# A two-layer decoder trunk on Trainium2: side-token gelu, index pieces and selection steps placed differently in the expert layers

## The chip, the core and the metric

The kernel runs on one core of one Trainium2 chip. The metric is the device time of one execution in microseconds (us). A core has five engines that run side by side, each with its own instruction queue worked off in order: PE (TensorE, matrix products), DVE (VectorE), ACT (ScalarE), POOL (GpSimd) and SP (SyncE, which here only issues transfers). DMA engines move data between HBM and the on-chip memory. An engine whose next instruction waits for another engine holds up everything behind it in its queue.

## What is computed

The reference is a trunk of two layers on 512 tokens of width 1024. Each layer has a mixer (gated linear attention in layer 1, stick-breaking attention in layer 2, both with cross-attention into 256 memory tokens) and a PEER expert layer, each followed by a layer norm. The change touches the expert layers alone. There, for each token:

```python
q = (xf @ w_q).reshape(N, PEER_HEADS, 2, PEER_QHALF)           # 8 heads, 2 halves of 128
s = jnp.einsum('nhpd,hpkd->nhpk', q, subkeys)                  # 128 scores per half
top_s, top_i = lax.top_k(s, PEER_TOPK)                         # 16 best of each half
cand_s = top_s[:, :, 0, :, None] + top_s[:, :, 1, None, :]     # 16 x 16 sums
best_s, best_pos = lax.top_k(cand_s.reshape(N, 8, 256), PEER_TOPK)
idx = jnp.take_along_axis(cand_i, best_pos, axis=-1)           # 128 experts of 16384
g = jax.nn.softmax(best_s, axis=-1)
act = jax.nn.gelu(jnp.einsum('nd,nhkd->nhk', xt, u_tab[it]))   # their products with x
out = jnp.einsum('nhk,nhkd->nd', gt * act, v_tab[it])          # weighted sum of v rows
```

## The kernel before, in words

**Two ways to the experts.** Tokens lie in four tiles of 128. For most tokens the kernel computes the products with *all* 16384 experts (the U stage, 128 blocks of 128 experts each), turns the chosen experts' weights into a dense matrix of gates, and multiplies by all rows of the V table (the V stage, 128 blocks). Tile 0, the gathered tile, instead fetches its 128 chosen rows per token with indirect DMA from POOL, from the U table and then from the V table. The first 16 tokens of tile 1, the side tokens, have their U products gathered too, but take part in the V stage. `SD` is 16, `T0` is 128 and `TU` is 368, the tokens whose U products are dense.

**The U stage.** The loop over `b` (L1605 on) issues for each block, in this order: `prep` loads the block two ahead and splits it into a high and a low part (`uh` on ACT, L97; `ul` on DVE, L98, issued a little later through `later`); `stat_mm` multiplies, 24 matmuls on PE (L117 to L119, tile `ph`); ACT applies gelu to the previous block's products (L1620 or L1622); then five streams of smaller work each get their share. A buffer ring of three holds the split parts.

**The streams.** A `Stream` holds generators and a credit `c`. A call adds a number of nanoseconds to `c` (at most twice that number stands there afterwards) and runs generator steps as long as `c` is above zero. Each step yields its assumed cost, which is subtracted; a step that yields `None` sets `c` to zero and ends the call. So the costs written in the `yield` lines decide in which block a piece is issued. The streams are:

- `gst`: the gates. Each step scales one-hot rows on ACT (`obl`, L1486), every second one makes new one-hot rows on DVE (`ob`, L1457 and L1463), and a step's products go to PE (`pg`, L1505 and L1506) one step later and through ACT (`gt`, L1509) to DRAM (`Gd`, L1511, issued from ACT's queue). The credit is 1.25 a block, so every fourth block has two steps. First come tile 1's gates without the side tokens, then the side tokens' (`side_gates`), then tiles 2 and 3.
- `lead`: the selection of the gathered tile. While the queries are made, `select` lets `topk16` work on one row of scores at a time for up to three tiles; after that `first_rest` does what is left: the last row (`stage1`), the last candidates (`stage2`), the indices of heads 4 to 7 (`indices`), and the softmax.
- `work`: the same for tiles 1, 2 and 3 (`rest`), with `gate_prep`, and `side_prep` for the side tokens. It runs only when `lead` is empty, with 1000 ns a block once gates can be made (`WB`), else 1700 (`WB0`).
- `gus`: the gathered products. A step of `gather_u` multiplies one gathered row per token on DVE (L1156, with its sum) and issues the next gather on POOL (L1103). After the last side product `side_late` is started, and each later step of `gather_u` runs it one `yield` further. `gather_v` follows, mostly in the V stage.

**Index operations.** `indices` turns positions among the candidates into expert numbers with fifteen short DVE operations (L1263 to L1278), then for four heads at a time two broadcasts on ACT (`tb`, L1286), two compares (L1290), two products (L1293) and a tree of sums (L1297, L1299) on DVE.

**`side_late`** applies gelu to the side products on ACT (L1384), multiplies by the softmax weights on DVE (L1386), sends them through DRAM (`Sw`, out and back on SP's queue) to another layout, transposes them on PE and makes three bf16 parts `wb`, for which `side_gates` waits.

**The V stage** (L1702 on) loads gates and V rows, forms `w` = gate times activation (L1694 on DVE, L1696 on ACT for the side tokens' gates), splits it (`whi` L1698, `wlo` L1699), splits the V rows, and multiplies into six accumulators (L285 to L289). Its first gates, those of U blocks 112 to 117, are loaded by SP into `g0`, a view of the tile the trace names `keep` or `big` (L1659). DVE, ACT and PE carry orders written out by hand inside each stage; a planner places the instructions of successive stages against each other, and orders SP's and POOL's.

Of the kernel before, what the change touches and what calls it, by code (L numbers as in the profile page):

```python
# [1052 lines left out]
def peer(E, mixer, wq, sk, ut, vt, un, lng, lnb, out_dram=None, follow=()):  # L1053
# [10 lines left out]
    with ExitStack() as pp:  # L1064
# [118 lines left out]
        with ExitStack() as up:  # L1183
# [8 lines left out]
            def topk16(*jobs):  # L1192

                for v, i, s, s2 in jobs:
                    nc.vector.max(v[:, 0:8], s)
                for v, i, s, s2 in jobs:
                    nc.vector.match_replace(s2, v[:, 0:8], s, -3.4e38)
                for v, i, s, s2 in jobs:
                    nc.vector.max_index(i[:, 0:8], v[:, 0:8], s)
                for v, i, s, s2 in jobs:  # L1200
                    nc.vector.max(v[:, 8:16], s2)
                for v, i, s, s2 in jobs:
                    nc.vector.max_index(i[:, 8:16], v[:, 8:16], s2)

            class Sel:
# [16 lines left out]

                def stage1(self):

                    topk16(*[self.job() for _ in range(min(2, avail[0] - self.nr))])
                    return 2350

                def stage2(self):

# [23 lines left out]
                def indices(self, h0=0, h1=8):  # L1253

                    n = (h1 - h0) * 16
                    ih = min(4, h1 - h0)
                    sh = wk.tile([P, P], U32, tag="sh", name="sh", bufs=1)[:, :n]
                    af = wk.tile([P, P], F32, tag="af", name="af", bufs=1)[:, :n]
                    bf = wk.tile([P, P], F32, tag="bf", name="bf", bufs=1)[:, :n]
                    ab = wk.tile([P, 2, P], F16, tag="ab", name="ab", bufs=1)  # L1260
                    st = sh.bitcast(F32)
                    tif = wk.tile([P, 16, 16], F16, tag="tif", name="tif", bufs=1)[:, 2 * h0:2 * h1]
                    nc.vector.tensor_copy(tif, self.top_i[:, 2 * h0:2 * h1])  # L1263
                    pf = self.pos[:, h0:h1].rearrange("p h k -> p (h k)")
                    nc.vector.tensor_scalar(sh, pf, 4, None, op0=ALU.logical_shift_right)
                    nc.vector.tensor_copy(af, sh)
                    nc.vector.tensor_scalar(sh, pf, 3, None, op0=ALU.logical_shift_right)
                    nc.vector.scalar_tensor_tensor(af, sh, -1.0, af, op0=ALU.add, op1=ALU.max)
                    nc.vector.tensor_scalar(sh, pf, 2, None, op0=ALU.logical_shift_right)
                    nc.vector.scalar_tensor_tensor(af, sh, -6.0, af, op0=ALU.add, op1=ALU.max)  # L1270
                    nc.vector.scalar_tensor_tensor(af, pf, -48.0, af, op0=ALU.add, op1=ALU.max)
                    nc.vector.tensor_scalar(st, af, 8.0, 8.0, op0=ALU.mult, op1=ALU.add)
                    nc.vector.scalar_tensor_tensor(bf, af, 16.0, st, op0=ALU.mult, op1=ALU.min)
                    nc.vector.tensor_scalar(st, af, 4.0, 24.0, op0=ALU.mult, op1=ALU.add)
                    nc.vector.tensor_tensor(bf, bf, st, op=ALU.min)
                    nc.vector.scalar_tensor_tensor(bf, af, 48.0, bf, op0=ALU.add, op1=ALU.min)
                    nc.vector.tensor_sub(ab[:, 1, :n], pf, bf)
                    nc.vector.tensor_copy(ab[:, 0, :n], af)  # L1278
                    yield 1000 + 10 * n
                    tv = tif.rearrange("p (h two) k -> p two h k", two=2)  # L1280
                    for h in range(0, h1 - h0, ih):
                        hs = slice(h, h + ih)
                        tb, eq = [], []
                        for half in range(2):
                            tb.append(wk.tile([P, 4, 16, 16], F16, tag=f"tb{half}", name="tb", bufs=1)[:, :ih])
                            nc.scalar.activation(tb[half], tv[:, half, hs, :, None].to_broadcast([P, ih, 16, 16]), AF.Copy)  # L1286
                        for half in range(2):
                            eq.append(wk.tile([P, 4, 16, 16], F16, tag=f"eq{half}", name="eq", bufs=1)[:, :ih])
                            av = ab[:, half, :n].rearrange("p (h k) -> p h k", k=16)
                            nc.vector.tensor_tensor(eq[half], av[:, hs, None, :].to_broadcast([P, ih, 16, 16]),  # L1290
                                                    E.iota16[:, None].to_broadcast([P, ih, 16, 16]), op=ALU.is_equal)
                        for half in range(2):
                            nc.vector.tensor_mul(eq[half], eq[half], tb[half])  # L1293
                        yield 700 * ih
                        for m in (8, 4, 2):
                            for e in eq:
                                nc.vector.tensor_add(e[:, :, 0:m], e[:, :, 0:m], e[:, :, m:2 * m])  # L1297
                        for half, e in enumerate(eq):
                            nc.vector.tensor_add(self.i12[:, half, h0 + h:h0 + h + ih], e[:, :, 0], e[:, :, 1])  # L1299
                        yield 500 * ih  # L1300
# [80 lines left out]
            def side_late():  # L1381

                sh, sg, sw = side["sh"], side["sg"], side["sw"]
                nc.scalar.activation(sh, sh, AF.Gelu)  # L1384
                yield
                nc.vector.tensor_mul(sh, sh, sg)  # L1386
                nc.sync.dma_start(Sw.rearrange("h t k -> (h t) k"), sh)
                for _ in range(3):
                    yield
                nc.sync.dma_start(sw[:SD].rearrange("t (h k) -> t h k", h=8), Sw.rearrange("h t k -> t h k"))  # L1390
                for _ in range(3):
                    yield
                pt = psum(E, name="gts")
                nc.tensor.transpose(pt[:, :SD], sw[:SD], E.ident[:SD, :SD])
                yield
                wb = tp.tile([P, 3, SD, 2], BF16, name="wb")
                ws = tp.tile([P, 2, SD], F32, name="ws")
                nc.vector.tensor_copy(ws[:, 0], pt[:, :SD])
                for k in range(3):
                    nc.vector.tensor_copy(wb[:, k], ws[:, 0, :, None].to_broadcast([P, SD, 2]))  # L1400
                    if k < 2:
                        nc.vector.tensor_copy(ws[:, 1], wb[:, k, :, 0])
                        nc.vector.tensor_sub(ws[:, 0], ws[:, 0], ws[:, 1])
                sready.append(wb)

            def side_gates():

                while not sready:
                    yield 1
                wb = sready[0]  # L1410
                pairs = lambda ap: ap.rearrange("p q (i two) -> p q i two", two=2)
                gt = wk.tile([P, P, TS], F32, tag="gt", name="gt")
                todo, ev = None, None
                for step in range(2 * SD // OT + 1):
                    n = step * OT // 2
                    if ev:
                        ev()
                        ev = None
                    if todo:
                        ev = side_mm(*todo)  # L1420
                        todo = None
                    elif n < SD:
                        if n % DT == 0:
                            ob = onehots(siT, None, n)
                        part = ob[:, n % DT:n % DT + OT]
                        e = pairs(part[:, :, 0])
                        ol = []
                        for k in (1, 2, 0):
                            o = e
                            if k > 0:  # L1430
                                ol.append(wk.tile([P, OT, P], F16, tag="obl", name="obl").bitcast(BF16))
                                o = pairs(ol[-1])
                            nc.vector.tensor_tensor(o, e, wb[:, k, n:n + OT, None, :].to_broadcast([P, OT, P // 2, 2]), op=ALU.mult)
                        todo = (n, gt, part, ol)
                    yield GR
# [79 lines left out]
            avail = [0]  # L1515
# [35 lines left out]
            lead = Stream()  # L1551
# [49 lines left out]
            avail[0] = 16  # L1601
            lead.q.append(first_rest())
            gst = Stream(gates(list(range(SD, P, OT))), side_gates(), gates(2 * list(range(0, P, OT))))
            ab, ph, later = None, None, []
            for b in range(P + 1):  # L1605
                if b == KB:
# [226 lines left out]
```

## Time and profile before

| | us |
|---|---|
| median of 3 runs | 2884.08 |
| lowest and highest run | 2877.16, 2887.15 |
| profiled execution, own time | 2882.44 |
| its span, first to last instruction | 2880.7 |
| PE busy | 2840.5 |
| DVE busy | 2407.6 |
| ACT busy | 1450.8 |

The U stage of layer 1 runs from 336 us to 913 us of the span, that of layer 2 from 1769 to 2346. In a timeline row the first number is the start in us from the span's beginning, the second the duration; then follow engine, line, operation, what it writes from what, the shapes, and how many such instructions the row merges. In square brackets stands how long the engine idled before it and what ended that. A row of waits reads: engine, waiting tile and line, what it waited for, us in total, how many times, the longest. A row of windows gives, after the stretch and its length, the busy time of PE, PE's weight loads, DVE, ACT and POOL, the granted clock of PE, the share of the DMA engines and GB/s.

### The profile page before, as it was taken

The numbers are of one execution on the slowest core, as the hardware profiler recorded it, in microseconds if no ns is written. First come the engines' busy times: TensorE is split into PE (matmuls) and PEld (weight loads), VectorE is DVE, ScalarE is ACT, GpSimd is POOL, SyncE is SP. The second block draws the span as 40 slices with busy tenths as digits, with TensorE's granted clock in tenths as the row PEclk, the third lists the DMA queues.
The fourth block names the chain that finished last, engine by engine and source line by source line (L and its number), as shares of the span: only waits on it lengthen the run. The fifth ranks groups of instructions, "written<-read, shape, count | busy, mean of one in ns | idle before, by whom it ended". The sixth has DMA issues, their size and how long they took to land. (4 is left out here: it accounts for less than half of the span.)

```text
span 2880.7 us, 44606 instructions
## 1 busy us (share of the span) xinstructions
PE 2840.5 (99%) x16144; PEld 2512.2 (87%) x16144; DVE 2407.6 (84%) x4944; ACT 1450.8 (50%) x2723; POOL 796.0 (28%) x584
## 2 busy tenths in 40 slices
PE   9999999999999999999999999999999999999998
PEld 7888899899999888888877788998999998888886
DVE  5567999899876888788868779998998778888888
ACT  6342447657674343344445424466676733344432
POOL 0100243233334333353000002432333333333330
PEclk9999999999999999999999999999999999999999
DMA  5232498899999999999521325988999999999994
GB/s 192 102 110 71 167 325 314 299 321 333 346 351 376 329 364 379 366 366 379 195 79 52 110 81 187 326 316 297 326 333 346 350 376 325 354 376 385 375 365 159
DMA packets 311070, 806.87 MB, mean 280 GB/s; under 512 B 32176, under 2 KB 124480, under 8 KB 304448
## 3 DMA queue, kind: packets, MB, share of 16 engines
q1 hardware_dynamic: 195936, 414.93, 41.3%
q0 software_dynamic: 78336, 285.25, 27.2%
q10 hardware_dynamic: 36576, 103.85, 9.4%
q8 instruction: 126, 2.06, 0.3%
q14 instruction: 96, 0.79, 0.1%
HBM read 708.19 MB, written 94.68 MB: 279 GB/s over the span
## 5 line engine op out<-in xcount | busy, mean ns | idle before, releaser
L117 PE MATMUL ph<-xhi,uh 128*128 128x368 f32 x2048 | 689.5, 337 | 0.0
L119 PE MATMUL ph<-xhi,ul 128*128 128x368 f32 x2048 | 677.5, 331 | 7.3 <-DVE ul L98 7.1
L118 PE MATMUL ph<-xlo,uh 128*128 128x368 f32 x2048 | 675.2, 330 | 0.0
L1103 POOL DMA_INDIRECT gr<-in_un,gidx x256 | 387.5, 1514 | 826.7 <-DVE gr L1156 599.4
L1103 POOL DMA_INDIRECT gr<-in_vt,gidx x256 | 334.7, 1307 | 610.5 <-DVE va L1175 530.3
L97 ACT ACTIVATE vh<-vr 128x1024 fp32r<-128x1024 f32 x256 | 271.2, 1060 | 427.7 <-PE acc L289 311.9
L285 PE MATMUL acc<-vh,whi 128*128 128x512 f32 x1536 | 473.8, 390 | 1.5 <-ACT whi L1698 1.5
L287 PE MATMUL acc<-vl,whi 128*128 128x512 f32 x1536 | 473.6, 389 | 0.1
L289 PE MATMUL acc<-vh,wlo 128*128 128x512 f32 x1536 | 473.3, 389 | 0.0
L98 DVE TENSOR_TENSOR vl<-vr,vh 128x1024 fp32r<-128x1024 f32 x256 | 313.0, 1223 | 157.4 <-ACT vh L97 156.0
L97 ACT ACTIVATE uh<-ur 128x1024 fp32r<-128x1024 f32 x288 | 303.9, 1055 | 204.4 <-PE ph L118 178.2
L119 PEld LDWEIGHTS ph<-xhi,ul 128*128 128x128 f32 x2048 | 386.1, 189 | 13.5 <-DVE ul L98 13.5
L98 DVE TENSOR_TENSOR ul<-ur,uh 128x1024 fp32r<-128x1024 f32 x288 | 351.1, 1219 | 47.7 <-ACT uh L97 46.4
L118 PEld LDWEIGHTS ph<-xlo,uh 128*128 128x128 f32 x2048 | 386.9, 189 | 0.0
L117 PEld LDWEIGHTS ph<-xhi,uh 128*128 128x128 f32 x2048 | 386.6, 189 | 0.1
L285 PEld LDWEIGHTS acc<-vh,whi 128*128 128x128 f32 x1536 | 287.6, 188 | 63.0 <-ACT whi L1698 3.7
L287 PEld LDWEIGHTS acc<-vl,whi 128*128 128x128 f32 x1536 | 287.8, 188 | 61.3 <-DVE vl L98 1.8
L289 PEld LDWEIGHTS acc<-vh,wlo 128*128 128x128 f32 x1536 | 287.7, 188 | 61.1 <-DVE wlo L1699 1.6
L1156 DVE SCALAR_TENSOR_TENSOR gr<-gr,xnat 128x1024 f32<-128x1024 f32 x256 | 310.0, 1217 | 24.8 <-DMA gr<-in_un,gidx 24.6
L1175 DVE SCALAR_TENSOR_TENSOR va<-gr,gw,va 128x1024 f32<-128x1024 f32 x254 | 325.1, 1280 | 3.8 <-DMA gr<-in_vt,gidx 2.7
L1486 ACT ACTIVATE obl<-ob,rat 128x128 f16<-128x128 f16 x736 | 234.3, 392 | 33.6 <-ACT gt L1509 16.2
L1698 ACT ACTIVATE whi<-w 128x384 fp32r<-128x384 f32 x256 | 132.2, 516 | 141.6 <-DVE w L1694 140.7
(358 smaller groups left out, 4100.0 us busy)
## 6 DMA issues: line engine op xcount, KB each, us to landing
ur<-in_ut SPq DMA_DIRECT2D x256, 512.0 KB
vr<-in_vt SPq DMA_DIRECT2D x256, 512.0 KB
Gd<-gt ACTq DMA_DIRECT2D x48, 1024.0 KB
Ad<-act ACTq DMA_DIRECT2D x112, 368.0 KB
al<-Ad SPq DMA_DIRECT2D x112, 368.0 KB
gl<-Gd SPq DMA_DIRECT2D x26, 1536.0 KB
ur<-in_wq SPq DMA_DIRECT2D x32, 512.0 KB
bs<-in_b_st SPq DMA_DIRECT2D x14, 512.0 KB
```

Of the source, the lines that this page charges most:

```text
L97: nc.scalar.activation(hi, raw, AF.Copy)
L98: sub = lambda: eng.tensor_sub(lo, raw, hi.bitcast(F32))
L117: nc.tensor.matmul(ps, h, xhi[:, c, sl], start=(c == 0), stop=False)
L118: nc.tensor.matmul(ps, h, xlo[:, c, sl], start=False, stop=False)
L119: nc.tensor.matmul(ps, l, xhi[:, c, sl], start=False, stop=(c == NC - 1))
L285: nc.tensor.matmul(acc[hf], lh, hi[:, hf * 512:(hf + 1) * 512], start=first, stop=False)
L287: nc.tensor.matmul(acc[hf], lh, lo[:, hf * 512:(hf + 1) * 512], start=False, stop=False)
L289: nc.tensor.matmul(acc[hf], ll, hi[:, hf * 512:(hf + 1) * 512], start=False, stop=last)
L1103: nc.gpsimd.indirect_dma_start(out=gr, out_offset=None, in_=tab, in_offset=bass.IndirectOffsetOnAxis(ap=idx[:, k:k + 1], axis=0))
L1156: nc.vector.scalar_tensor_tensor(gr, gr, 1.0, xr, op0=ALU.mult, op1=ALU.mult, accum_out=dst[:, k:k + 1])
L1175: nc.vector.scalar_tensor_tensor(va, gr, gw[:, k:k + 1], va, op0=ALU.mult, op1=ALU.add)
L1486: nc.scalar.activation(obl[:, q], ob[:, q, 0], AF.Copy, scale=rat[:, n0 + q:n0 + q + 1])
```

## The change

Four things are done. In `side_late` two more `yield` lines stand ahead of the gelu, so it is issued two steps of `gather_u` later. In `indices` the fifteen operations are cut in two pieces of eight and seven, the compares and the products become pieces of their own, and the assumed costs are other numbers. In `stage1` the assumed cost goes by the number of rows, 1200 ns each, instead of 2350 for any number. And ahead of the U loop the credit of `lead` is set to -2000, whatever it was.

```diff
                 def stage1(self):
-                    topk16(*[self.job() for _ in range(min(2, avail[0] - self.nr))])
-                    return 2350
+                    jobs = [self.job() for _ in range(min(2, avail[0] - self.nr))]
+                    topk16(*jobs)
+                    return 1200 * len(jobs)
...
                     nc.vector.scalar_tensor_tensor(af, pf, -48.0, af, op0=ALU.add, op1=ALU.max)
+                    yield 700 + 11 * n
                     nc.vector.tensor_scalar(st, af, 8.0, 8.0, op0=ALU.mult, op1=ALU.add)
...
                     nc.vector.tensor_copy(ab[:, 0, :n], af)
-                    yield 1000 + 10 * n
+                    yield 600 + 10 * n
...
                                                     E.iota16[:, None].to_broadcast([P, ih, 16, 16]), op=ALU.is_equal)
+                        yield 300 * ih
                         for half in range(2):
                             nc.vector.tensor_mul(eq[half], eq[half], tb[half])
-                        yield 700 * ih
+                        yield 300 * ih
...
                 sh, sg, sw = side["sh"], side["sg"], side["sw"]
+                yield
+                yield
                 nc.scalar.activation(sh, sh, AF.Gelu)
...
             gst = Stream(gates(list(range(SD, P, OT))), side_gates(), gates(2 * list(range(0, P, OT))))
+            lead.c = -2000.0
             ab, ph, later = None, None, []
```

Here `n` is 16 times the number of heads (128 for a whole tile, 64 for half) and `ih` is 4.

## Prediction

> **What bounds the kernel now.** I read the page first, then the list of waits on TensorE, then the timelines of TensorE, ScalarE and VectorE around the longest of these waits.
>
> ```profile
> span 2880.7 us, 44606 instructions
> PE 2840.5 (99%) x16144; PEld 2512.2 (87%) x16144; DVE 2407.6 (84%) x4944; ACT 1450.8 (50%) x2723; POOL 796.0 (28%) x584
> ```
>
> TensorE sets the time, and the change gives it no less to do. What can be won is only what TensorE loses to waits and to a slow clock. Who makes it wait:
>
> ```profile
> PE pg L1506 <- ACT obl L1486: 9.4, 4, 4.4
> PE ph L119 <- DVE ul L98: 7.1, 11, 1.5
> ```
>
> Both names lie in the stage the change edits (blocks b = 0 to 127 of the U loop, once in each layer). The first wait, in layer 1, at block 40:
>
> ```profile
> 507.99 0.42 PE L117 MATMUL ph<-xhi,uh 128*128 128x368 f32 x1
> ...
> 517.10 0.29 PE L1506 MATMUL pg<-ob,obl 128*128 128x128 f16 x1 [4.33 <-ACT obl L1486]
> ...
> 518.02 0.65 PE L117 MATMUL ph<-xhi,uh 128*128 128x368 f32 x1
> ...
> 524.52 0.41 PE L117 MATMUL ph<-xhi,uh 128*128 128x368 f32 x1
> ...
> 529.04 0.42 PE L117 MATMUL ph<-xhi,uh 128*128 128x368 f32 x1
> ...
> 533.56 0.41 PE L117 MATMUL ph<-xhi,uh 128*128 128x368 f32 x1
> ...
> 538.53 0.41 PE L117 MATMUL ph<-xhi,uh 128*128 128x368 f32 x1
> ```
>
> These are the first matmuls of blocks 40, 41, 42, 43, 44 and 45, with the wait between. A block with one gate step takes 529.04 - 524.52 = 4.52 us, one with two takes 538.53 - 533.56 = 4.97. Block 40 (two steps) took 518.02 - 507.99 = 10.03 and block 41 (one step) 524.52 - 518.02 = 6.50: lost 5.06 + 1.98 = **7.04 us**, of which 4.33 are the wait and the rest a slower clock after it. Layer 2 has the same:
>
> ```profile
> 1941.38 0.42 PE L117 MATMUL ph<-xhi,uh 128*128 128x368 f32 x1
> ...
> 1951.43 0.65 PE L117 MATMUL ph<-xhi,uh 128*128 128x368 f32 x1
> ...
> 1958.02 0.42 PE L117 MATMUL ph<-xhi,uh 128*128 128x368 f32 x1
> ```
>
> 10.05 and 6.59, so 5.08 + 2.07 = 7.15 us. Why ScalarE is late is in its timeline and in that of VectorE:
>
> ```profile
> 505.09 1.28 ACT L1486 ACTIVATE obl<-ob,rat 128x128 f16<-128x128 f16 x4
> 513.71 0.22 ACT L1384 ACTIVATE sh<-sh 128x16 f32<-128x16 f32 x1 [7.34 <-DVE gr L1156]
> ```
> ```profile
> 508.38 0.29 DVE L1263 CAST tif<-top_i 128x256 f16<-128x256 uint32 x1
> ...
> 510.28 0.29 DVE L1271 SCALAR_TENSOR_TENSOR af<-pos,af 128x128 f32<-128x128 uint32 x1
> ...
> 512.45 1.22 DVE L1156 SCALAR_TENSOR_TENSOR gr<-gr,xr 128x1024 f32<-128x1024 f32 x1
> ```
>
> The gelu of the side tokens (L1384) stands in ScalarE's queue and waits 7.34 us for the last side product (the L1156 at 512.45). That product stands on VectorE behind all fifteen index operations of tile 2, 508.38 to 512.45 = 4.07 us. Behind the gelu stand the split of the next block, the activation, the gate copy and the scaled one-hots `obl` for which TensorE stops.
>
> **The early waits.** The second list entry is mostly blocks 3 to 5:
>
> ```profile
> 343.74 0.33 PE L117 MATMUL ph<-xhi,uh 128*128 128x368 f32 x1
> ...
> 347.74 0.33 PE L117 MATMUL ph<-xhi,uh 128*128 128x368 f32 x1
> ...
> 349.16 0.44 PE L119 MATMUL ph<-xhi,ul 128*128 128x368 f32 x1 [0.93 <-DVE ul L98]
> ...
> 354.89 0.44 PE L119 MATMUL ph<-xhi,ul 128*128 128x368 f32 x1 [1.46 <-DVE ul L98]
> ...
> 359.58 0.43 PE L119 MATMUL ph<-xhi,ul 128*128 128x368 f32 x1 [0.41 <-DVE ul L98]
> ...
> 363.35 0.33 PE L117 MATMUL ph<-xhi,uh 128*128 128x368 f32 x1
> ```
> ```profile
> 1781.10 0.33 PE L117 MATMUL ph<-xhi,uh 128*128 128x368 f32 x1
> ...
> 1796.74 0.33 PE L117 MATMUL ph<-xhi,uh 128*128 128x368 f32 x1
> ```
>
> A block without gates takes 347.74 - 343.74 = 4.00. Blocks 3 to 5 took 363.35 - 347.74 = 15.61 instead of 12.00, and 15.64 in layer 2: **3.61 + 3.64 us** lost. VectorE is still busy with the gathered tile's selection there:
>
> ```profile
> 342.89 0.29 DVE L1195 MAX8 top_s<-sall 128x8 f32<-128x128 f32 x1
> ...
> 346.76 1.20 DVE L1156 SCALAR_TENSOR_TENSOR gr<-gr,xnat 128x1024 f32<-128x1024 f32 x1
> ...
> 347.89 1.22 DVE L98 TENSOR_TENSOR ul<-ur,uh 128x1024 fp32r<-128x1024 f32 x1
> 349.03 0.22 DVE L1263 CAST tif<-top_i 128x128 f16<-128x128 uint32 x1
> ...
> 352.47 1.22 DVE L1156 SCALAR_TENSOR_TENSOR gr<-gr,xnat 128x1024 f32<-128x1024 f32 x1
> ```
>
> The `ul` at 347.89 is block 3's. Ahead of it lie the last selection step pair, 342.89 to 346.76 = 3.87 us (issued in block 0); behind it the index operations, 349.03 to 352.47 = 3.44 us (block 1), ahead of block 4's `ul`.
>
> **The change, part by part.** No engine gets more or fewer instructions. Only positions in VectorE's and ScalarE's queues move, and the DMA issues that hang on them.
>
> *Gelu two gather steps later.* One gather step is made per block here. By the streams' arithmetic (1000 ns of credit a block once gates run, each piece subtracts what it yields) the last side product moves from block 39 to block 41, and the gelu to the end of block 43. VectorE then has ScalarE's whole blocks 42 and 43, two times 4.52 = 9.0 us, more than the 7.34 it was late, and only the first eight index operations (508.38 to about 510.57, 2.2 us) stand ahead of the product. So I take the gelu's wait as zero, and with it both losses: -7.04 - 7.15 = **-14.2 us**. The gelu itself (0.22 us) lies in ScalarE's slack (1450.8 of 2880.7 us busy). If a part of the wait stayed, the `obl` of block 44, again one with two gate steps, would be late. Behind the gelu the product with `sg`, the `Sw` store and load on SP's queue, the transpose and the weights move along: the weights come in block 51, the side gates start in block 52 instead of 50.
>
> *Lead stream set to -2000.* Block 0 gets no selection step; the pair comes in block 1, behind block 3's `ul`, the index operations in block 3, behind block 5's. By hand from the rows: block 0's product ends at 344.0, block 3's `ul` at 345.2 (needed at 348.1), pair and product to 350.2, block 4's `ul` at 351.4 (needed at 352.1), product to 352.6, block 5's at 353.7 (needed at 356.1), indices and product to 358.3, block 6's at 359.5 (needed at 360.1). No wait is left, though the margins are 0.6 to 3 us: **-7.2 us** for both layers. If half of the wait came back, it would be 3.6.
>
> *Smaller pieces, truer costs.* A tile's full index work is now charged 2108 + 1880 = 3988 instead of 2280 (the row says 4070), the two one-hot passes 2400 instead of 2800 each, a selection pair 2400 instead of 2350. Work on VectorE is spread more evenly, but each tile is ready later. Followed to the end, tile 3's last gate step moves from block 118 to block 121. The small waits left in the two list entries, 9.4 - 4.33 - 4.35 = 0.7 and 7.1 - 5.6 = 1.5 us (5.6: twice the 0.93, 1.46 and 0.41 of blocks 3 to 5), may go or come: the 0.7 is behind an index block of tile 3, which is now split, so I take -0.7; for the 1.5, around blocks 52 to 60, zero, with -1.5 and +8 as ends (next rival).
>
> *What is late next* is the end of the U stage. The V stage's first gates are loaded from what the gate steps store:
>
> ```profile
> 872.53 0.41 PE L117 MATMUL ph<-xhi,uh 128*128 128x368 f32 x1
> ```
> ```profile
> 874.75 0.33 ACTq L1511 DMA_DIRECT2D Gd<-gt  x1
> ...
> 894.76 0.22 ACT L1696 ACTIVATE w<-keep 128x16 f32<-128x16 f32 x1 [8.69 <-DMA keep<-Gd]
> ...
> 902.29 1.06 ACT L97 ACTIVATE uh<-ur 128x1024 fp32r<-128x1024 f32 x1 [1.14 <-DMA ur<-in_ut]
> ```
> ```profile
> 895.96 1.22 DVE L98 TENSOR_TENSOR ul<-ur,uh 128x1024 fp32r<-128x1024 f32 x1 [0.74 <-ACT uh L97]
> ```
> ```profile
> 913.83 0.73 PE L285 MATMUL acc<-vh,whi 128*128 128x512 f32 x2 [0.41 <-ACT whi L1698]
> ```
>
> The last store is issued at 874.75, 2.2 us into block 118 (872.53), and `w` of V block 0 runs 20.0 us later. In the queues `w` stands ahead of the last four U splits, those of blocks 124 to 127 (the last starts at 902.29), though the code issues it after them; the `ul` at 895.96 is block 124's. The V stage begins 913.83 - 874.75 = 39.1 us after the store. In the changed order the store comes just after block 121's products, 0.7 us into block 122: four blocks of 4.0 less 1.5 = 14.5 us later. `w` would be ready 14.5 + 20.0 = 34.5 us after today's place of the store, still 4.6 us ahead of the V stage. Whether TensorE feels it depends on where `w` stands. Behind the last split: nothing, and today's 0.4 us of wait at the V start may vanish. Ahead of the last one: `w` is ready 0.6 us into block 127, its `uh` and `ul` follow (1.06 + 1.22), and the block starts about 2.7 us late. As the store and `w` should move by nearly the same number of blocks, I take +1 a layer, **+2 us**, with -0.8 and +5.4 as ends.
>
> The sum: -14.2 - 7.2 - 0.7 + 2.0 = -20.1 us on the profiled execution, whose own time is 2882.4 (span 2880.7): 2862.3. The median of the runs shown is 2884.1, 1.6 above it, so the forecast is **2864.0 us**.
>
> The clock: in the 4 us after the wait it was half.
>
> ```profile
> 516.00:520.00 4.00, 2.90 (x13) 2.43 (x14) 3.50 (x6) 3.60 (x11) 0.94 (x1) 0.50 1.01 329
> ```
>
> By the Trainium skill (TensorE: Matmul & The Clock Gate, "Part 1: The HAM clock gate") an idle window of some 3.4 us drops the clock to half and about as long a busy stretch restores it, which makes an estimated 1.7 us of loss per gap instead of the 2.7 measured here; the gain would then be 2 us smaller and the time 2866. The trace agrees that 4.33 us of idling halves the clock; the measured blocks decide the size.
>
> **The rivals.** *(a) The late `w` keeps its place ahead of four splits.* ScalarE and VectorE would stand at it until 894.76 + 14.5 = 909.3, the split of block 124 and its `ul` would follow at about 911.5 instead of 897.2, and TensorE would idle 14.3 us and run slowly after it (2.7, as above): 17 a layer, +34 against -22, **2896 us**, slower. It decides from the point where the waiting `w` stands more than one split ahead of its data. For it: today's order already puts it ahead of data (8.69 us of waiting). Against it: the same planner orders the moved store. If it stands two splits ahead, the idling is 6.7 + 2.7 a layer and the time 2881.
>
> *(b) VectorE bunches around blocks 52 to 60.* Side one-hots, softmax and a selection pair of tile 3 fall into block 52, more side one-hots, the gate preparation of tile 2 and two gather products into block 56. Such stretches gave the 1.5 us of small waits; four times that in each layer, 4 to 5 us more, gives 2873.
>
> *(c) The gelu still stalls*, because VectorE is a further block behind than I count. Then only the early waits go, 2877. Against it: before the index operations VectorE was one product behind (7.34 - 4.07 - 1.2 - 1.1 for product and `ul` is about 1 us).
>
> **How the numbers follow.** Forecast 0.70; (a) in full 0.06, two splits 0.08; (b) 0.08; (c) 0.07; rest 0.01. Changes under 0.3% (8.7 us, about what a measurement of this kernel can tell) are "same": the half-way form of (a) and (c), less what might lie just outside, make 0.13; (a) in full makes 0.06 slower; forecast and (b) with the rest 0.81 faster. The range runs from 2856 (no cost at the V start, all small waits gone, and the 3 us by which runs differ) to 2877 (the far end of (c)).
>
> **What would show it.** Right: no wait over 1 us at L1506 near 500 to 530 and 1930 to 1960, no granted clock of 0.95 in those slices of the page, the gelu's wait for `gr` below 1 us, blocks 3 to 5 at 4.0 us, PE busy time down by about 5 us (slow clock) and span by about 20. Wrong: a wait for `ul` or `whi` of several us between 880 and 915 with ScalarE idle for `keep<-Gd`, or `pg` waits that moved to blocks 44 and 52 to 60.

## The result, and the profile after

The changed kernel takes **2861.2 us** (median of four runs, 2858.8 to 2862.5) against 2884.3 for the kernel before beside it: a ratio of 0.9923, 95% interval 0.9903 to 0.9942. The gain is 23.1 us; the forecast was 2864.0, a gain of 20.1. One execution of the run with the store early (below) took 4011 us at a granted clock of 0.65, in a slow state of the chip, and is left out of every figure.

The head of the page after, and the list of waits on TensorE (waiting tile and line, what it waited for, us in total, times, the longest):

```profile
span 2857.1 us, 44575 instructions
PE 2829.1 (99%) x16144; PEld 2507.4 (88%) x16144; DVE 2410.4 (84%) x4944; ACT 1445.3 (51%) x2723; POOL 778.2 (27%) x584
```
```profile
PE acc L285 <- ACT whi L1704: 4.5, 5, 2.5
PE bsp L133 <- DVE bsl L98: 1.6, 2, 1.1
PE pg L1446 <- DVE ob L1438: 1.6, 2, 0.8
PE ph L119 <- DVE ul L98: 1.2, 2, 0.6
```

(The inserted lines shift the numbers: `obl` is now L1491, its products L1511, the gelu L1389, `w` L1700 on DVE and L1702 on ACT, `whi` L1704.) The 9.4 us of waiting for `obl` have no row any more, and the waits for `ul` fell from 7.1 to 1.2 us. What grew is the wait for `whi`, from 1.5 to 4.5, and 1.6 us of waiting for `ob` in block 59 are new. The profiled execution took 2858.8 us, and its span fell by 2880.7 - 2857.1 = 23.6.

The first matmuls of blocks 40, 41, 43, 44 and 45 of layer 1, then the last side product on VectorE and the gelu on ScalarE:

```profile
503.15 0.41 PE L117 MATMUL ph<-xhi,uh 128*128 128x368 f32 x1
...
508.12 0.42 PE L117 MATMUL ph<-xhi,uh 128*128 128x368 f32 x1
...
517.16 0.41 PE L117 MATMUL ph<-xhi,uh 128*128 128x368 f32 x1
...
521.68 0.42 PE L117 MATMUL ph<-xhi,uh 128*128 128x368 f32 x1
...
526.66 0.41 PE L117 MATMUL ph<-xhi,uh 128*128 128x368 f32 x1
```
```profile
514.17 0.29 DVE L1264 CAST tif<-top_i 128x256 f16<-128x256 uint32 x1
...
516.27 1.22 DVE L1156 SCALAR_TENSOR_TENSOR gr<-gr,xr 128x1024 f32<-128x1024 f32 x1
```
```profile
520.15 0.20 ACT L1389 ACTIVATE sh<-sh 128x16 f32<-128x16 f32 x1
```

Blocks 40 and 44 take 4.97 and 4.98, block 43 takes 4.52: nothing is lost. The gelu stands at the end of block 43, carries no bracket, and starts 2.7 us after its product has ended (517.5). Ahead of the product lie eight index operations (514.17 to 516.27 = 2.1 us), not fifteen.

Blocks 3 to 5, and what is left of the small waits, in block 59:

```profile
347.74 0.33 PE L117 MATMUL ph<-xhi,uh 128*128 128x368 f32 x1
...
359.74 0.33 PE L117 MATMUL ph<-xhi,uh 128*128 128x368 f32 x1
...
590.21 0.44 PE L119 MATMUL ph<-xhi,ul 128*128 128x368 f32 x1 [0.58 <-DVE ul L98]
...
594.95 0.23 PE L1446 MATMUL pg<-ob 128*128 128x128 bf16 x1 [0.80 <-DVE ob L1438]
```

359.74 - 347.74 = 12.00 for three blocks. Now the end of the U stage, in layer 1 on ScalarE and TensorE, in layer 2 on VectorE and TensorE, with the clock behind it:

```profile
877.47 0.33 ACTq L1516 DMA_DIRECT2D Gd<-gt  x1
...
888.74 1.06 ACT L97 ACTIVATE uh<-ur 128x1024 fp32r<-128x1024 f32 x1 [2.58 <-PE ph L118]
...
897.17 0.21 ACT L1702 ACTIVATE w<-keep 128x16 f32<-128x16 f32 x1 [7.01 <-DMA keep<-Gd]
...
908.11 9.38 ACTq L1665 DMA_DIRECT2D gl<-Gd  x1
```
```profile
901.24 0.73 PE L285 MATMUL acc<-vh,whi 128*128 128x512 f32 x2 [0.37 <-ACT whi L1704]
...
919.17 0.73 PE L285 MATMUL acc<-vh,whi 128*128 128x512 f32 x2 [0.93 <-ACT whi L1704]
```
```profile
2319.97 1.23 DVE L1156 SCALAR_TENSOR_TENSOR gr<-gr,xnat 128x1024 f32<-128x1024 f32 x1 [1.76 <-DMA gr<-in_un,gidx]
...
2321.12 0.54 DVE L1700 TENSOR_TENSOR w<-keep 128x368 f32<-128x368 f32 x1
```
```profile
2322.32 0.88 PE L285 MATMUL acc<-vh,whi 128*128 128x512 f32 x2 [2.53 <-ACT whi L1704]
```
```profile
2320.00:2322.00 2.00, 0.00 (x0) 0.00 (x0) 2.00 (x4) 0.26 (x1) 0.52 (x1) 1.00 1.02 407
2322.00:2324.00 2.00, 1.68 (x5) 1.26 (x6) 2.00 (x4) 1.87 (x5) 0.47 (x1) 0.69 1.01 400
2324.00:2326.00 2.00, 2.00 (x6) 1.52 (x5) 1.95 (x4) 1.92 (x5) 0.00 (x0) 0.50 1.04 409
```

`w` on ScalarE now stands *behind* the last split of the U stage (888.74), 19.7 us after the store, 4.1 us ahead of the V stage. In layer 2 the first V product is late by 2.53 us because VectorE's part of `w` (2321.12) stands behind gathered products that wait for their transfers, and the clock is half for a while behind it. ScalarE's issue of the next gates (908.11) holds its queue for 9.38 us; the `whi` behind it costs the 0.93.

Where the 23.6 us are, from the first U matmul to the last block's last L117 ("U stage"), on to the first V matmul, and on:

| stretch | before, us | after, us | difference |
|---|---|---|---|
| U stage, layer 1 | 577.10 | 564.56 | -12.54 |
| U stage, layer 2 | 577.37 | 564.66 | -12.71 |
| U to V, both layers | 1.08 + 1.07 | 1.03 + 3.19 | +2.07 |
| V stage 1 to U stage 2 | 855.18 | 853.23 | -1.95 |
| V stage 2 to the end, and the start | 868.90 | 870.43 | +1.5 |

### The profile page after: what moved, and what is told of

Its sections match the earlier page's. It is cut to its first block, busy times and chain, and to the rows that moved or that the text cites. A ratio compares the mean times of both kernels' runs of the same rounds, so it can differ in the third digit from the quotient of the medians.

```text
span 2857.1 us, 44575 instructions
## 1 busy us (share of the span) xinstructions
PE 2829.1 (99%) x16144; PEld 2507.4 (88%) x16144; DVE 2410.4 (84%) x4944; ACT 1445.3 (51%) x2723; POOL 778.2 (27%) x584
## 5 line engine op out<-in xcount | busy, mean ns | idle before, releaser
L117 PE MATMUL ph<-xhi,uh 128*128 128x368 f32 x2048 | 687.7, 336 | 0.0
L1103 POOL DMA_INDIRECT gr<-in_vt,gidx x256 | 311.8, 1218 | 646.9 <-DVE va L1175 553.4
L117 PEld LDWEIGHTS ph<-xhi,uh 128*128 128x128 f32 x2048 | 385.1, 188 | 0.1
L1491 ACT ACTIVATE obl<-ob,rat 128x128 f16<-128x128 f16 x736 | 234.1, 392 | 38.0 <-DVE ob L1468 18.3
L1704 ACT ACTIVATE whi<-w 128x384 fp32r<-128x384 f32 x256 | 131.1, 512 | 78.5 <-DVE w L1700 78.1
```

The source lines that it names most:

```text
L117: nc.tensor.matmul(ps, h, xhi[:, c, sl], start=(c == 0), stop=False)
L1103: nc.gpsimd.indirect_dma_start(out=gr, out_offset=None, in_=tab, in_offset=bass.IndirectOffsetOnAxis(ap=idx[:, k:k + 1], axis=0))
L1491: nc.scalar.activation(obl[:, q], ob[:, q, 0], AF.Copy, scale=rat[:, n0 + q:n0 + q + 1])
```

## The experiments

The theory, as the prediction has it: the gelu's two steps bring 14.2 us, the lead's credit 7.2, the pieces 0.7, and the later store costs 2; the terms add up. The rivals: the parts take away one and the same stop, so that they don't add up; and the later store is what the V stage waits for. G, L and P name the two `yield` lines, the lead's credit, and the pieces with their costs. All eight combinations ran, and beside them two other places of the store and one other cut of the pieces. Each ratio is to the kernel before as it ran beside that kernel: its median was 2882.9 for G, L, G+L and L+P, 2881.3 for P and the two stores, 2882.8 for the rest, so gains and ratios compare better than medians. "U stage" is both layers against before, from the profiled executions.

| kernel | median, us | ratio to before, 95% | U stage, us |
|---|---|---|---|
| G | 2874.9 | 0.9969 (0.9956 to 0.9981) | -10.3 |
| L | 2870.9 | 0.9958 (0.9944 to 0.9972) | -7.8 |
| P | 2873.2 | 0.9973 (0.9963 to 0.9982) | -10.3 |
| G, L | 2859.5 | 0.9921 (0.9907 to 0.9935) | -19.9 |
| L, P | 2862.5 | 0.9929 (0.9915 to 0.9943) | -22.8 |
| G, P | 2865.4 | 0.9936 (0.9923 to 0.9950) | -17.7 |
| G, L, P (the change, again) | 2861.5 | 0.9921 (0.9908 to 0.9935) | -25.3 |
| the change, store early | 2857.6 | 0.9918 (0.9903 to 0.9932) | -24.6 |
| the change, store late | 2888.6 | 1.0026 (1.0017 to 1.0035) | -25.5 |
| store early, compares joined | 2857.0 | 0.9910 (0.9895 to 0.9925) | -22.7 |

**G alone.** To the kernel before:

```diff
                 sh, sg, sw = side["sh"], side["sg"], side["sw"]
+                yield
+                yield
                 nc.scalar.activation(sh, sh, AF.Gelu)
```

> The kernel before with the two later gelu steps and nothing else. Additive theory (the prediction's sum): the gelu's wait for `gr` (7.34 us) goes, and with it the `pg` stop of 4.3 us and the slow clock in each layer, -14.2; the early waits of blocks 3 to 5 (-7.2 in the change) and the 1.1 us at block 81 stay: about 2870. Rival (the parts need each other): the gelu is two steps later but VectorE's index work still comes in one piece of 4 us, so part of the stop moves to block 44, the next one with two gate steps: about 2 us of `pg` wait there in each layer, and only about -8: 2876.

2874.9 us, the rival's number, but not its mechanism: the wait at block 44 is 0.2 us and not 2. The gelu (521.89) doesn't wait any more, and where 7.04 us were lost 0.88 are: block 44 takes 5.85 instead of 4.97. So the term for the gelu's stop is right to within 1 us a layer. What is missing was lost later in the profiled execution. At the end of the U stage in layer 2, on ScalarE and TensorE:

```profile
2296.48 0.33 ACTq L1513 DMA_DIRECT2D Gd<-gt  x1
...
2318.05 0.22 ACT L1698 ACTIVATE w<-keep 128x16 f32<-128x16 f32 x1 [10.24 <-DMA keep<-Gd]
```
```profile
2319.28 0.43 PE L117 MATMUL ph<-xhi,uh 128*128 128x368 f32 x1 [0.50 <-ACT uh L97]
...
2320.53 0.44 PE L119 MATMUL ph<-xhi,ul 128*128 128x368 f32 x1 [0.67 <-DVE ul L98]
```

`w` stands ahead of four splits, as before, but came 21.6 us after the store instead of 19.9 (the same layer before), and U blocks waited behind it. In the V stage ScalarE stood at a transfer of layer-norm weights:

```profile
2602.55 0.35 ACTq L1013 DMA_DIRECT2D gam<-in_lng  x1
...
2612.51 0.20 ACT L1006 ACTIVATE junk<-gam 128x1 f32<-128x1 f32 x1 [7.81 <-DMA gam<-in_lng]
```
```profile
2614.23 0.73 PE L285 MATMUL acc<-vh,whi 128*128 128x512 f32 x2 [2.67 <-ACT whi L1700]
```

The load took 10.0 us from issue to use; before it took 8.2 (layer 1) and 8.3 and stopped nobody. This execution took 2877.7 us, in a spread of 2871.0 to 2877.9; what the other executions lost, and where, no trace shows.

**L alone.** To the kernel before:

```diff
+            lead.c = -2000.0
             ab, ph, later = None, None, []
```

> The kernel before with only the lead stream's credit set to -2000. Additive theory: blocks 3 to 5 take 4.00 us each, -3.6 a layer, the gelu's stop stays as long as it was (4.3 us of `pg` wait and a slow clock in each layer): -7.2, about 2877. Rival: the lead's delay moves every gathered product two blocks, so the gelu meets another place in VectorE's queue; the stop could shrink below the length that slows the clock (-10 to -14 in all, 2870 to 2874) or, behind one more selection pair, grow (2880).

2870.9 us, inside the rival's span, but not by its mechanism. Blocks 3 to 5 don't wait. The gelu still waits 5.74 us, and TensorE stops twice instead of once:

```profile
522.96 0.23 PE L1506 MATMUL pg<-ob,obl 128*128 128x128 f16 x1 [0.95 <-ACT obl L1486]
...
531.28 0.23 PE L1506 MATMUL pg<-ob,obl 128*128 128x128 f16 x1 [2.63 <-ACT obl L1486]
```

The three blocks around take 6.18 + 8.32 + 6.09 = 20.59 instead of 14.01 (4.52 + 4.97 + 4.52), so 6.6 us are lost of 7.0: 3.58 are these waits, 1.70 the slow clock behind the second. The U stage gains 7.8, as the additive theory has it. The profiled execution was the slowest of five (2875.8 us, with a stop of 3.02 us in the V stage, see the end), so where the rest of the gain lies isn't settled. One part is outside the U stage: in the kernel before TensorE waits 1.62 us for `lny` and 1.75 for `bsl` ahead of the mixer of layer 2, with a slow clock behind; with L the first is gone and the second is 1.12.

**G and L, no pieces.** Both edits above.

> The kernel before with the later gelu and the lead's credit, but the index operations and selection pairs in their old pieces and costs. Additive theory: the pieces are worth 0.7 us or nothing, and since the last store comes one block earlier than in the full change, the start of the V stage loses less: -21.4 to -24, 2860 to 2863, no slower than the full change. Rival: the smaller pieces are what lets the last side product through; without them a `pg` wait of 2 us or more is at block 44 and `ul` waits at 52 to 60: 2868 or more.

2859.5 us, 23.4 below the kernel before beside it: the additive theory, which said 21.4 to 24. As fast as the full change, although a `ul` wait of 1.55 us at block 59 is left in each layer. Its U stage is 5.4 us longer than the full change's, and it gets this back later: its waits for `whi` are 1.1 us in all, where the full change has 4.5.

**L and P, no later gelu.** To the kernel after:

```diff
                 sh, sg, sw = side["sh"], side["sg"], side["sw"]
-                yield
-                yield
                 nc.scalar.activation(sh, sh, AF.Gelu)
```

> The full change without the two later gelu steps. Additive theory: the gelu's stop is back in full, 4.3 us of `pg` wait and a slow clock in each layer, +14.2 on the full change's 2861: 2875. Rival: seven of the fifteen index operations (about 2 us) no longer lie ahead of the last side product and the lead's credit shifts it, so the gelu waits about 4 us instead of 7.3, the `pg` stop is under 2 us and the clock stays whole: +2 to +5, 2863 to 2866.

2862.5 us: the rival. ScalarE and TensorE, in block 44:

```profile
517.17 0.22 ACT L1387 ACTIVATE sh<-sh 128x16 f32<-128x16 f32 x1 [3.77 <-DVE gr L1156]
```
```profile
526.53 0.23 PE L1509 MATMUL pg<-ob,obl 128*128 128x128 f16 x1 [0.44 <-ACT obl L1489]
...
526.82 0.23 PE L1509 MATMUL pg<-ob,obl 128*128 128x128 f16 x1
...
527.11 0.23 PE L1509 MATMUL pg<-ob,obl 128*128 128x128 f16 x1
```

The gelu waits for the last side product still, 3.77 instead of 7.34 us, because seven of the fifteen index operations no longer stand ahead of it. ScalarE's slack holds nearly all of that: TensorE stops 0.44 us and the clock stays whole. Block 44 still takes 6.12 instead of 4.97 us, 1.15 more: behind the stop the products come at the pace at which ScalarE scales their `obl`, 0.29 us apart instead of 0.11. So of the 14.2 us that the prediction put on the two `yield` lines, all but 1.2 to 1.3 us a layer (565.73 and 565.97 against 564.56 and 564.66) come without them, once L and P are there.

**P alone.** To the kernel after, both of the above taken out:

```diff
-                yield
-                yield
                 nc.scalar.activation(sh, sh, AF.Gelu)
...
-            lead.c = -2000.0
```

> The kernel before with only the smaller pieces and the new costs (index operations, selection pairs); the gelu and the lead's credit as before. Additive theory: the early waits and the gelu's stop stay, -0.7 and +2 at the V stage's start: 2884 to 2886. Rival (the pieces alone take index operations out of the gelu's way): the gelu's wait falls to about 5.6 us and its `pg` stop to 3.5, which may leave the clock whole: -4 to -8, 2876 to 2880.

2873.2 us, 8.1 below the kernel before beside it: the rival's mechanism, at the upper end of its gain. The gelu waits 5.38 us, TensorE 2.37:

```profile
514.95 0.23 PE L1509 MATMUL pg<-ob,obl 128*128 128x128 f16 x1 [2.37 <-ACT obl L1489]
```

The two blocks lose 4.65 instead of 7.04 us (8.05 + 6.09 against 4.97 + 4.52), clock included: it was not left whole. Block 81, split now, loses nothing instead of 6.06 - 4.97 = 1.09. The early waits are one of 2.60 in block 3 and one of 0.31 in block 6, and blocks 3 to 6 lose 3.45 us instead of 3.61. These make 7.4 of the 10.3 us in the U stages; small losses gone from other blocks make most of the rest.

**G and P, no lead.**

```diff
-            lead.c = -2000.0
             ab, ph, later = None, None, []
```

> The full change without the lead stream's credit of -2000. Additive theory: blocks 3 to 5 lose 3.6 us again in each layer, +7.2 on the full change: about 2868. Rival (the parts overlap): with the index operations in two pieces the early wait is about 2 us at block 4 alone, as the 2.6 us in the run with the pieces alone, and the last store comes two blocks earlier, which takes the waits at the start of the V stage away: +1 to +3, 2861 to 2864.

2865.4 us, between the two. One early wait of 2.65 us is left in block 3 (2.67 in layer 2), with half the clock for 3.4 us behind it in both; nothing waits for `whi` at the start of the V stage.

**The store early.** To the kernel after; the last gates are prepared earlier, their store comes 11.4 us earlier in the U stage:

```diff
-                yield 4000
+                yield 0
                 yield from prev.gate_prep()
```

> The full change with the assumed cost after the last selection 0 instead of 4000, so that the last gates are prepared and stored two blocks earlier (the place of the first side gates and all else unchanged). Theory (the late store is what the start of the V stage waits for): the store is 8 to 9 us earlier, the waits of 0.37 and 0.93 us at the V stage's start in layer 1 and of 2.53 us with a clock of 0.73 to 0.84 behind it in layer 2 go, -4 to -5: 2856 to 2857. Rival: these waits come from the gathered products and gate loads that fall there anyway: no change, 2860 to 2862.

2857.6 us, 23.6 below the kernel before beside it, where the change gained 23.1 and, run again, 21.2; the ratios (0.9918 against 0.9923 and 0.9921) differ by less than their intervals. Of the waits on TensorE for `whi` the list keeps

```profile
PE acc L285 <- ACT whi L1704: 0.7, 2, 0.3
```

instead of 4.5; a wait of 0.99 for `vl` at the V start of layer 1 came in. The theory's mechanism is borne out, since the waits go with the later store. Its 4 to 5 us are not: what is gained is 0.5 to 2.4, not clear of the noise.

**The store late.** The same line with 9000:

```diff
-                yield 4000
+                yield 9000
                 yield from prev.gate_prep()
```

> The full change with the assumed cost after the last selection 9000 instead of 4000, so that the last store comes three blocks later (some 13 us). Theory: `w` of the first V block comes 19.7 us after the store; in the full change that was 4.1 us ahead of the V stage in layer 1 and 5.5 in layer 2, but already with waits, so nearly the whole 13 us is idle time of TensorE in each layer, and the clock is slow behind it: +24 to +32, 2885 to 2893, slower than before. Rival: other work (the U blocks' rest, gathered products) fills part of it: +10, 2871.

2888.6 us, 7.4 above the kernel before beside it, so 29 to 31 above the change. ScalarE, TensorE, and the clock:

```profile
886.20 0.33 ACTq L1516 DMA_DIRECT2D Gd<-gt  x1
...
910.61 0.22 ACT L1702 ACTIVATE w<-keep 128x16 f32<-128x16 f32 x1 [13.19 <-DMA gr<-in_vt,gidx]
```
```profile
912.60 1.22 PE L285 MATMUL acc<-vh,whi 128*128 128x512 f32 x2 [11.69 <-ACT whi L1704]
```
```profile
912.00:914.00 2.00, 1.40 (x3) 1.16 (x4) 2.00 (x4) 1.60 (x4) 0.00 (x0) 0.50 0.18 72
...
918.00:920.00 2.00, 2.00 (x9) 1.63 (x8) 0.06 (x1) 0.17 (x1) 0.00 (x0) 0.84 1.04 348
```

8.7 us later in the store (886.20 against 877.47) are 11.7 us of idle time, since `w` now comes 24.4 us after it, and 10.4 in layer 2. From the U to the V stage the two layers take 23.4 us instead of 4.2; slow clock behind it (3.0 and 2.8 us) and waits in the V stage (3.00) and the mixer (2.93), with a slow clock behind the latter, make up the rest. The store of the full change thus lies just where its margin ends.

**Compares and products joined, store early.**

```diff
-                        yield 300 * ih
                         for half in range(2):
                             nc.vector.tensor_mul(eq[half], eq[half], tb[half])
-                        yield 300 * ih
+                        yield 700 * ih
```

> The full change with the early store (0 instead of 4000) and with compares and products of the index work in one piece again (700 a head, one `yield`), the fifteen operations still cut in two. Theory: the `ul` and `pg` waits at block 59 (0.6 and 0.8 us and a slower block after them, about 1.8 us a layer in the full change) come from where the split compares fall; joined, they fall away or shrink to 1 us: 1 to 2 us below the early store alone, 2855 to 2857. Rival: the bunch at block 59 is the side gates' one-hots whatever the pieces are: 2858, as the early store alone.

2857.0 us. The waits at block 59 are gone but for 0.2 us in block 61, as the theory has it; yet the U stage is 0.8 to 1.1 us a layer longer than with the early store alone: a wait of 0.52 at L1340 and others further on take their place. In time it can't be told from the early store alone. It has the lowest median of all, 4.6 us below the change beside it (2856.97 and 2861.54).

> The full change as it is, on the same chip as the two beside it, to compare them: 2860 to 2862, ratio 0.992 to 0.993.

2861.5 us, ratio 0.9921, as the first time. Its profile has the same U stages within 0.1 us, but TensorE's waits for `whi` are 7.5 us in all and not 4.5: 1.39 and 2.47 at the V start of layer 1, 1.10 and 1.84 in layer 2. So the loss at the V start comes in both, and its size and place differ between executions of one kernel.

## Why the prediction was right, and where it was not

**The gelu's stop, -14.2: right as an effect, wrong as a cause.** The blocks lose nothing any more in either layer, and the gelu is where it was put, behind the product that has eight index operations ahead of it. That 7 us a layer went *because of the two steps* is what the runs deny. With L and P there the steps bring 1.2 to 1.3 us a layer in the U stage; alone they bring 7.04 - 0.88 = 6.2 at this place. Each of the three parts shortens this one stop, the lead's credit least (6.6 us are left), and the prediction gave it to one. The size came out because the stop goes whichever of them take it away.

**The early waits, -7.2: right.** Blocks 3 to 5 take 12.00 us. L alone shows the same.

**The pieces, -0.7: the step that failed.** "The 0.7 is behind an index block of tile 3, which is now split, so I take -0.7": that block lost 1.09 a layer, not its wait of 0.38, since the products behind the wait came at ScalarE's pace as in the run without the later gelu; and P alone brings 10.3 us in the U stage. In the full sum this was hidden, since its largest effect, the shorter stop of the gelu, was counted under G already. The U stage went by 7.04 + 3.61 + 1.09 = 11.74 in layer 1 and 7.15 + 3.64 + 1.09 = 11.88 in layer 2; most of the 0.8 left of each (12.54, 12.71) lies in small losses that are gone from blocks 13, 124 and 127 (0.26, 0.41 and 0.23 in layer 1), which the sum didn't have. Blocks 45 to 63 take 86.14 us before and 86.16 after in layer 1, so the zero for blocks 52 to 60 was right.

**The end of the U stage, +2.0: right in place, short in size, another engine.** The store came when forecast (`w` 4.1 us ahead of the V stage, 4.6 expected), and `w` on ScalarE stood behind the last split, the case priced at nothing. But the V start waited: +2.07 to the first V matmul in both layers, 0.93 shortly after in layer 1, and 1.7 us of slow clock in layer 2, 4.7 in all (7.7 by the same count in the run of the change again). The late instruction of layer 2 is VectorE's `w`, which the prediction didn't name.

The sum was 20.1, the span went by 23.6: -25.25 in the U stages against -22.1, +4.7 for +2.0, and some 3 us between the layers that weren't in the sum. That these errors partly cancel is luck. PE's busy time fell by 11.4 us instead of about 5; the slow clock of the two gaps explains 5.4 of it, and the rest isn't settled. These 3 us (the -1.95 of the table without the 0.93 that it holds) go with the waits for `lny` and `bsl`, which are shorter in every run with L but the one with the late store; what sets them stays open.

**The rivals.** (a), the late `w`: the way it was priced, idle time and 2.7 us of slow clock, held where the store is 9 us later (11.69 + 3.0 and 10.39 + 2.8); its condition did not come about; in G alone a small form did. (b), the bunch at blocks 52 to 60: it is there, in block 59, with waits of 1.38 us instead of 0.63, at no cost in the sum of these blocks. (c), the stalling gelu: not with G; with L and P but without G the gelu waits 3.77 us and TensorE 0.44.

**The clock.** The prediction set 2.7 us a gap against an estimated 1.7 by the Trainium skill (TensorE: Matmul & The Clock Gate, "Part 1: The HAM clock gate"). At the gaps of 4.33 us it was 2.7; at shorter ones, below, it is 1.70, where there is any.

## What to carry to other kernels

When several parts of a change work on the queue ahead of one late instruction, price each alone and each against the others: a stop can be taken away three times and is gained once. A stop can cost more than its wait: here 4.33 us cost 7.04, since the clock was half behind it, and 0.44 cost 1.15, since the next products came at the slower engine's pace. A wait within the slack of the engine behind it costs next to nothing, so half of a cure may be nearly all of it. After a stage is made faster and its last store later, look for the first consumer of the next stage on *every* engine, and try an earlier store: here it took these waits away, though the time gained isn't clear of the noise.

## What the runs showed of the hardware

**The clock falls behind gaps much shorter than 4 us, but not always.** Of the gaps of TensorE in these twelve traces, from the U stage of layer 1 on, none of fifteen between 1.30 and 1.62 us slowed it, sixteen of twenty-three between 1.75 and 3.02 us did, and all four of 4.33 and more. One of 1.12 us did too, in the run without the later gelu, close behind waits of 0.55 and 0.48. The gaps of 1.75 to 3.02 that counted cost 1.70 us each, sixteen times (nine windows of 1 us, one minus the granted clock, summed), the long ones 2.6 to 3.0. In the run with P alone a gap of 2.60 us left the clock whole and one of 2.37 did not:

```profile
349.00:351.00 2.00, 0.00 (x0) 0.00 (x0) 2.00 (x4) 1.52 (x3) 0.84 (x1) 1.00 0.00 0
351.00:353.00 2.00, 1.92 (x11) 1.92 (x12) 1.83 (x9) 0.00 (x0) 0.83 (x1) 1.00 0.42 115
...
513.00:515.00 2.00, 0.05 (x1) 0.06 (x2) 2.00 (x3) 1.19 (x4) 0.47 (x1) 1.00 0.68 214
515.00:517.00 2.00, 1.98 (x13) 1.47 (x14) 1.60 (x4) 2.00 (x7) 0.94 (x1) 0.93 1.01 329
517.00:519.00 2.00, 2.00 (x9) 2.00 (x8) 1.68 (x3) 2.00 (x5) 0.00 (x0) 0.50 1.02 424
```

What decides is how a gap lies on a grid in time. The slow stretches of one run start whole steps of 3.413 us apart: in the kernel before at 515.53, 1454.20 and 1949.13, which are 275 and 145 steps. If TensorE's idle time is added up in each step of a run's grid, all eighteen steps at full clock with 1.75 us or more of it are followed by a slow one, three of eight with 1.60 to 1.74, and none with less. The gap of 2.60 us above is cut by the grid into 1.00 and 1.60; of the one of 2.37, 1.63 lie in one step, which has 1.65 in all. So the limit lies near half a step.

The Trainium skill (TensorE: Matmul & The Clock Gate, "Part 1: The HAM clock gate") has a window of some 3.4 us that runs on its own, whatever the kernel does. The grid, and that 1.70 is half of 3.4, agree with it; that a whole idle window is needed does not, since half of one was enough.

**A transfer waited for in ScalarE's queue can stop TensorE in one execution and not in another.** The layer-norm weights take about 8 us from issue to use, and ScalarE stands for 5.5 to 6.3 of them in the V stage, with TensorE waiting 0.4 us at most, in 22 of 24 places; at 7.81 us TensorE stopped for 2.67 us and its clock fell. In L alone a wait of 5.62 us at the same place cost 3.02, with splits that waited for V rows around it. Such a stop is 4.4 to 4.7 us with the clock (2.67 + 1.70, 3.02 + 1.70), as much as lies between the runs of one kernel; that it makes this spread was not tried.
